# Later loads, split stores and readings, and a later meeting of q and k in a two-layer decoder kernel

## The chip, the cores and the metric

The kernel runs on one core of one Trainium2 chip. Its time is the device time of one execution in microseconds, the median of the runs shown. A core has a matrix engine (PE, with its weight loads listed apart as PEld), a vector engine (DVE), a scalar engine (ACT), a general one (POOL) and an engine that here only issues transfers (SP). Each of them executes its own instructions in the order in which the program emits them; semaphores tie them together.

## The reference

Two decoder layers over 256 positions of width 2048, in float32, with a final RMSNorm. Each layer norms its input, multiplies it by one wide input matrix, mixes the heads, gates the result and multiplies it by an output matrix:

```python
def layer_even(x, norm_g, w_in, w_out):        # layer 0
    h = rmsnorm(x, norm_g)
    qa, ka, va, iq, ik, iw, qb, kb, vb, gate = split_cols(h @ w_in, SPLIT0)
    ...                                        # rotary embedding of q and k
    o_a = dsa_attention(qa, ka, va, iq, ik, iw)    # 10 heads, 64 keys chosen by an indexer
    o_b = dilated_attention(qb, kb, vb)            # 6 heads, three dilated windows merged
    y = concatenate([o_a, o_b])
    return x + (y * silu(gate)) @ w_out

def layer_odd(x, norm_g, w_in, b_f, w_out):    # layer 1
    h = rmsnorm(x, norm_g)
    qc, kc, vc, qd, kd, vd, fl, gate = split_cols(h @ w_in, SPLIT1)
    o_c = stick_breaking_attention(qc, kc, vc)     # 8 heads
    o_d = forgetting_attention(qd, kd, vd, log_f)  # 8 heads, softmax with forget bias
    y = concatenate([o_c, o_d])
    return x + (y * silu(gate)) @ w_out
```

All heads are 128 wide. The weights are about 160 MB of float32 and are read once.

## The kernel before

**Projections.** The work is a list of 39 jobs (lines 228 to 231): 14 of layer 0 (B0, K, I0, I1, B1 and so on; a B job is one head's q, k, v and gate, 512 columns; an A job is the q and gates of two heads; K holds the shared key and value, I0 and I1 the indexer's queries), four output jobs P0 to P3, 17 of layer 1 (C and D heads, with C1 cut in F1 and G1 of about half width), and Q0 to Q3. `project` runs a job over 16 blocks of the contraction (kt) for both halves of the positions (th). Precision comes from splitting every operand in a high and a low part, so each block takes six matmuls: lines 316, 317 and 319, twice. The weights arrive in pieces of four blocks (1 MB at full width) in three buffers with the tag "raw" (line 252). `split` cuts half a piece at a time: ACT writes the high part `whi` (line 280), DVE the low part `wlo` (line 281), each in four buffers. The splits run three halves ahead of the matmuls (`AHEAD`, line 310). When the second half of a piece has been put in line, `split` calls `load` for a further piece (line 284).

**Ticks.** Everything else is woven into the projections by hand. A piece of side work is a generator that yields the number of ticks it wants to wait; a tick is one block of a job at full width, six matmuls (lines 304 to 308 and 336). `advance` resumes the generators that are due, oldest first. So a tick sets only the place of an instruction in its engine's queue; when it executes is up to the queue and the semaphores. In these pages, tick 0 of a head is the end of its projection, and tick 16 is the end of the next one of full width.

**A head.** At tick 0 the head's opening work takes q, k, v and the gate out of PSUM (`scaled_qk`, `vg1` in layer 1; `rotate` in layer 0). q and k have to be turned (transposed) for their product, and so has the gate u. That goes through DRAM, by `far` (line 400): DVE transposes blocks of 32 by 32 (line 410), a store writes them out (line 411), a reading brings them back in the wanted order (line 413). `qk_turned` then cuts q and k in parts (`qk_parts`, ACT lines 388 and 389, DVE line 390), which is called "parts" below; A heads do the same in lines 709 to 711. One or two ticks later q meets k in a matmul (line 486 for A, B and D, line 853 for C). What follows in a softmax head is the row minimum and exponential (`soft`, lines 492 and 494), `share`, the turning of the weights on PE (`turn`, line 380), the cut into ph and pl, and `weigh_out`, which multiplies with v and with the turned gate and writes the head's columns of y. A C head (`stick_head`) has a logarithm and a running sum by matmul (lines 865 to 868) in the place of the softmax.

In ticks of a D head, before the change: qk transposed and stored at 2, u at 5, qk read back at 5, u at 9, parts at 9, meeting at 10, weigh_out at 17. Heads A and B meet at 11. The last heads before an output job, B5 and D7 (`last`), turn q and k on PE instead, and their gate through DRAM with shorter waits.

**Transfers.** Nearly all of them are issued by SP, in order: loads of weights, stores and readings of turned blocks, the residual x (lines 259 and 260). An instruction at the head of SP's queue that waits holds those behind it. Several tiles share a tag with few buffers: "qk" has two (q and k of a head, the indexer's `iqr`, the key `kr`, the turned residual `xf`).

**feed1** (line 761) turns the residual after each P job the same way, as input of layer 1, and **keys_a** (line 601) the shared key of the A heads.

Of the kernel before, what the change touches and what calls it, by code (L numbers as in the profile page):

```python
# [14 lines left out]
P = 128  # L15
# [31 lines left out]
def _run_of(base, h):  # L47
    return np.arange(base + h * HD, base + (h + 1) * HD)
# [11 lines left out]
def _cols0(n):  # L60
    qa, ka, va, iq, ik, iw, qb, kb, vb, g = O0
    h = int(n[1:] or 0)
    if n == "K":
        p = [_inter(ka, HD), _run_of(va, 0), _inter(ik, DI), np.arange(iw, iw + NI)]
    elif n[0] == "I":
        p = [_inter(iq + (8 * h + i) * DI, DI) for i in range(8)]
    elif n[0] == "B":
        p = [_inter(qb + h * HD, HD), _inter(kb + h * HD, HD), _run_of(vb, h), _gate_of(g, HA + h)]
    else:
        p = [_inter(qa + h * HD, HD), _inter(qa + (h + 1) * HD, HD), _gate_of(g, h), _gate_of(g, h + 1)]  # L70
    return np.concatenate(p)


def _cols1(n):
    qc, kc, vc, qd, kd, vd, fl, g = O1
    h = int(n[1:])
    if n[0] == "F":
        p = [_run_of(qc, h), _run_of(kc, h), np.arange(fl, fl + HDD)]
    elif n[0] == "G":
        p = [_run_of(vc, h), _gate_of(g, h)]  # L80
    elif n[0] == "C":
        p = [_run_of(qc, h), _run_of(kc, h), _run_of(vc, h), _gate_of(g, h)]
    else:
        p = [_run_of(qd, h), _run_of(kd, h), _run_of(vd, h), _gate_of(g, HC + h)]
    return np.concatenate(p)


# [84 lines left out]
def trunk(ctx, tc, x, xT, g1, w0, wo0, w1, wo1, bf, gf, consts, rope, out):  # L172
# [68 lines left out]
    def load():  # L241
        i = st["load"]
        if i == len(pieces):
            return
        st["load"] += 1
        wd, off, n, w = pieces[i]
        if i < len(FIRST):

            kt = sum(FIRST[:i])
            raws[i] = home[kt // 8][:, (kt % 8) * w:(kt % 8 + n) * w]  # L250
        else:
            raws[i] = wp.tile([P, n * w], F32, name="raw", tag="raw")
        if i == 1 or 3 < i < len(FIRST):
            load_xT(kt)
        nc.sync.dma_start(raws[i], wd[off:off + P * n * w].rearrange("(p f) -> p f", p=P))
        if i in (0, 2):
            load_xT(i)
        if i == len(FIRST) + 1:
            for th in range(NT):
                nc.sync.dma_start(xs[:, th, :], x[th * P:(th + 1) * P, :])  # L260
            nc.sync.dma_start(rt.rearrange("p a b -> p (a b)"), rope)
        if i == len(FIRST) + 2:
            nc.sync.dma_start(cons, consts)

    def split(upto):
        while st["split"] < min(upto, len(halves)):
            i = st["split"]
            st["split"] += 1
            ji, pi, kt, j0, m = halves[i]
            w = pieces[pi][3]  # L270
            if jobs[ji][2] == "Q3" and kt < 8:
                hi = xh.rearrange("p a b -> p (a b)")[:, kt * w:(kt + m) * w]
                lo = xl.rearrange("p a b -> p (a b)")[:, kt * w:(kt + m) * w]
            else:
                hi = wp.tile([P, m * w], F32R, name="whi", tag="whi", bufs=4)
                lo = wp.tile([P, m * w], F32R, name="wlo", tag="wlo", bufs=4)
            if ji == 0:
                feed0(kt, m)
            rw = raws[pi][:, j0 * w:(j0 + m) * w]
            nc.scalar.activation(hi, rw, AF.Copy)  # L280
            nc.vector.tensor_tensor(lo, rw, hi.bitcast(F32), op=OP.subtract)  # L281
            parts[i] = (hi, lo)
            if (i + 1 == len(halves) or halves[i + 1][1] != pi) and (pi >= len(FIRST) - 1 or kt + m == 10):
                load()


    side = []
# [16 lines left out]
    def tick(w):  # L304
        clock["t"] += w / 512
        if clock["t"] >= 0.99:
            clock["t"] -= 1.0
            advance(1)

    AHEAD = 3  # L310
    hidx = [0]
# [85 lines left out]

        return t.rearrange("p (i b c) -> p b i c", i=4, b=n)

    def far(srcs, dst, first, between):  # L400

        yield first
        t = hp.tile([P, 512], F32, name="far", tag="rt2")
        ns = [x.shape[1] // P for x in srcs]
        n = sum(ns)
        d = dr.tile([P, P * n], F32, name="fard", tag=f"fard{n}", bufs=4)
        o = t[:, 0:P * n].rearrange("p (j b c) -> p b j c", j=4, b=n)
        for i, x in enumerate(srcs):
            b = sum(ns[:i])
            nc.vector.transpose(o[:, b:b + ns[i]], x.rearrange("p (b j l) -> p b j l", j=4, l=32))  # L410
        nc.sync.dma_start(d, t[:, 0:P * n])
        yield between
        nc.sync.dma_start(dst.rearrange("p (i f) -> p i f", i=4),
                          d.rearrange("r (j f) -> (r j) f", j=4).rearrange("(i q) f -> q i f", i=4))

    def qk_turned(qk, first, last):

        if last:
            yield first + 1
            r = qk_parts(quarters(turn([qk[:, i * P:(i + 1) * P] for i in range(4)])))  # L420
            yield 1
        else:
            yield from far([qk], qk, first, 3)
            yield 4
            r = qk_parts(arrived(qk, 4))
        yield 1
        return qk_of(r)

# [31 lines left out]
            upper(th)  # L460
        return (vh, vl, v1), upper, lower

    def gate_turned(u, last=False, n=NT):
        uT = hp.tile([P, P * n], F32, name="uT", tag="uT" if n == NT else "rl")
        start(far([u], uT, 1 if last else 5, 3 if last else 4))
        return arrived(uT, n)

    def weigh_out(ph, pl, p1, v, uT, kt, swap):

# [37 lines left out]
        for th, s in BLK:  # L507
            nc.vector.tensor_scalar(pr[:, s], pr[:, s], sc[:, th:th + 1], None, op0=OP.mult)

    def softmax_head(qk, nb, v, uT, rs, kt, last):  # L510
        pr, l = soft(qk, nb)
        yield 2
        share(pr, factor(l, rs))
        yield 2 if last else 3
        pt = turn([pr[:, 0:P], pr[:, P:SEQ], pr[:, SEQ:384]])
        ph = hp.tile([P, SEQ], F32R, name="ph", tag="ph", bufs=1)
        pl = hp.tile([P, SEQ], F32R, name="pl", tag="pl", bufs=1)
        p1 = hp.tile([P, P], F32, name="p1", tag="p1", bufs=1)
        cut((ph, pl), pt[:, 0:SEQ])
        nc.scalar.activation(p1, pt[:, SEQ:384], AF.Copy)  # L520
        yield 2
        weigh_out(ph, pl, p1, v, uT, kt, False)

# [56 lines left out]
    def head_b(ps, h):  # L580
        qk = hp.tile([P, 512], F32, name="qk", tag="qk")
        v, upper, lower = values(ps, 256, r0, ())
        u = hp.tile([P, SEQ], F32, name="u", tag="u")
        tg = hp.tile([P, SEQ], F32, name="tg", tag="tg")
        for th in range(NT):

            rotate(qk[:, th * 256:(th + 1) * 256], ps[th][:, 0:256], rt[:, th, 0:256], rt[:, th, 256:512], 1, 256,
                   swap=th == 1)
            o = 1 - th
            nc.scalar.activation(tg[:, o * P:(o + 1) * P], ps[o][:, 384:512], AF.Tanh, scale=hr0[:, o:o + 1])  # L590
            upper(o)
        for th in (1, 0):
            t = slice(th * P, (th + 1) * P)
            nc.vector.scalar_tensor_tensor(u[:, t], tg[:, t], 1.0, ps[th][:, 384:512], op0=OP.add, op1=OP.mult)
        lower()
        last = h == HB - 1
        uT = gate_turned(u, last)
        t = yield from qk_turned(qk, 3, last)
        yield from softmax_head(t, bmask, v, uT, hr0, YPOS[f"B{h}"], last)

    def keys_a(ps):
        kr = hp.tile([P, 512], F32, name="kr", tag="qk")
# [11 lines left out]
        for j in range(2):  # L614
            d = slice(j * DI, (j + 1) * DI)
            c = slice(SEQ + j * P, SEQ + (j + 1) * P)
            for t in (ikh, ikl):
                nc.gpsimd.tensor_copy(t[d, c], t[d, 0:P].bitcast(F32))
        yield from far([kr[:, 0:256]], kr[:, 0:256], 1, 3)
        yield 4  # L620
        k = arrived(kr[:, 0:256], 2)
        nc.scalar.activation(quarters(kA), k[:, 0:1], AF.Copy)
        nc.scalar.activation(quarters(kAh), k, AF.Copy)
# [66 lines left out]
    def heads_a(ps, h):  # L690
# [7 lines left out]
        for th in (1, 0):  # L698
            nc.vector.scalar_tensor_tensor(u[:, :, th, :], tgs[th].rearrange("p (a b) -> p a b", a=2), 1.0,
                                           ps[th][:, 256:512].rearrange("p (a b) -> p a b", a=2),  # L700
                                           op0=OP.add, op1=OP.mult)
        uT = gate_turned(u.rearrange("p a b c -> p (a b c)"), n=4)
        yield from far([qk], qk, 3, 3)
        yield 4
        q = arrived(qk, 4)
        f = hp.tile([P, 256], F32, name="qqf", tag="qkf", bufs=1)
        hi = hp.tile([P, 256], F32R, name="qqh", tag="qkh", bufs=1)
# [1 line left out]
        nc.scalar.activation(quarters(hi), q[:, 2:4], AF.Copy)  # L709
        nc.scalar.activation(quarters(f), q[:, 0:2], AF.Copy)  # L710
        nc.vector.tensor_tensor(quarters(lo), q[:, 2:4], quarters(hi).bitcast(F32), op=OP.subtract)
        yield 1
        js = [slice(j * P, (j + 1) * P) for j in range(2)]

        ph, pl = (hp.tile([P, 2, SEQ], F32R, name="pA" + n, tag="i" + n, bufs=1) for n in "hl")
# [45 lines left out]
    def feed1(ps, c):  # L761
        residual(ps, 1, c)
        us = [hp.tile([P, 512], F32, name="xf", tag="qk") for _ in range(2)]
        for i, t in enumerate(us):
            k = (c * 4 + 2 * i) * P
            start(far([xs[:, th, k:k + 2 * P] for th in range(NT)], t, 1 + i, 3))
        yield 4
        if c == 3:
            norm(1)
# [108 lines left out]

    def stick(qk, v, u, kt):
        uT = gate_turned(u)  # L880
        t = yield from qk_turned(qk, 2, False)
        yield from stick_head(t, v, uT, kt)

    def head_c(ps, h):
# [8 lines left out]
    def head_d(ps, h):  # L893
        qk = scaled_qk(ps, 1, (0, 3), (1, 2))
        v, u = vg1(ps, 256)
        last = h == HDD - 1
        uT = gate_turned(u, last)
        t = yield from qk_turned(qk, 2, last)
        yield from softmax_head(t, biases[h], v, uT, None, HC + h, last)


    def tail(ps, c2):
# [131 lines left out]
```

## Time and profile before

| what | value |
|---|---|
| median of the runs shown | 1050.57 us (1042.25 to 1053.46) |
| the profiled execution, its own time | 1054.77 us |
| its span, first to last instruction | 1053.0 us |
| mean granted clock of PE in it | 0.942 |
| DMA moved | 194.72 MB, mean 185 GB/s |
| instructions | 11945 |

The profile belongs to one execution. Its views list, for each engine, the busy time (a busy PE is not a PE at full speed, since it also counts matmuls at a lower clock), groups of instructions by source line with count, total and mean duration, who waited for whom, and the instructions in order of time. A row of the timeline reads: start, duration, engine, line, operation, output and input tile, shapes, count, and in square brackets how long the engine had been idle and what released it. A row of the table of stretches reads: from and to, length, busy time with the number of instructions for PE, PEld, DVE, ACT and POOL, then PE's granted clock, the busy share of the DMA engines, and GB/s. In the list of waits a row reads: engine, waiting tile and line, what it waited for, total us, times, longest.

### The profile page before, as it was taken

Reading aid. Unit: us, or ns where it says so; the run is one execution under the profiler, and the core shown is the slowest. Engines: PE = TensorE matmul, PEld = TensorE weight load, DVE = VectorE, ACT = ScalarE, POOL = GpSimd, SP = SyncE. Lnnn points to the kernel's source line nnn. Section 1 sums busy time; section 2 is a strip of 40 time slices with the busy share of each in tenths; the row PEclk is TensorE's granted clock in tenths of the full one; section 3 lists DMA queues with packets and bytes.
Section 4 is the critical chain, followed back from the end, with each engine's and each line's share of the span. In section 5 each row is a group of like instructions: output and inputs, shape, how many; then the busy total and the mean of one; then the engine's idle time right before and its main releaser. Section 6 shows DMA issues by size and latency. Waiting matters only on the chain.

```text
span 1053.0 us, 11945 instructions
## 1 busy us (share of the span) xinstructions
PE 941.6 (89%) x4291; PEld 778.1 (74%) x4291; DVE 651.9 (62%) x1138; ACT 481.6 (46%) x832; POOL 50.2 (5%) x71
## 2 busy tenths in 40 slices
PE   9999998998988899999978889887878977879997
PEld 6878877776767688878866667776666766767886
DVE  6678877566666666667645566564556644657554
ACT  6645544444444455454544444444333433445441
POOL 0131000000000000000000000000000000000010
PEclk9999999999999999999988899898889888989999
DMA  9944455556555546665655553445655346454452
GB/s 368 342 161 158 156 203 174 179 195 200 200 166 194 190 156 206 210 239 170 233 190 156 184 190 127 150 150 195 197 185 166 125 140 191 158 185 166 171 193 80
DMA packets 68123, 194.72 MB, mean 185 GB/s; under 512 B 16976, under 2 KB 39904, under 8 KB 49888
## 3 DMA queue, kind: packets, MB, share of 16 engines
q1 hardware_dynamic: 66624, 190.66, 53.4%
q0 software_dynamic: 864, 2.12, 1.2%
q10 hardware_dynamic: 576, 1.19, 0.3%
q8 instruction: 33, 0.54, 0.2%
q14 instruction: 26, 0.21, 0.1%
HBM read 178.87 MB, written 15.08 MB: 184 GB/s over the span
## 4 chain that ended last, share of the span: by engine, by line
PE 43%; DMA 29%; DVE 14%; ACT 9%; issue 5%; SPq 0%; POOL 0%; DVEq 0%; POOLq 0%; ACTq 0%
DMA qk<-fard 14%; PE pj L316 13%; PE pj L317 12%; PE pj L319 12%; DMA fard<-far 10%; DVE wlo L281 5%; ACT whi L280 3%; DVE e L805 3%; DVE far L410 2%; DMA xf<-fard 2%; PE s L486 1%; DMA xs<-in_x_dram 1%; DMA raw<-in_w_in_dram 1%; ACT e L802 1%; ACT qkh L388 1%
## 5 line engine op out<-in xcount | busy, mean ns | idle before, releaser
L281 DVE TENSOR_TENSOR wlo<-raw,whi 128x1024 fp32r<-128x1024 f32 (+3 forms) x300 | 355.2, 1198 | 141.6 <-ACT whi L280 139.0
L316 PE MATMUL pj<-whi,xh 128*128 128x512 f32 (+3 forms) x992 | 396.8, 401 | 0.2
L317 PE MATMUL pj<-whi,xl 128*128 128x512 f32 (+3 forms) x992 | 391.9, 396 | 0.0
L280 ACT ACTIVATE whi<-raw 128x1024 fp32r<-128x1024 f32 (+3 forms) x300 | 300.0, 1023 | 108.6 <-PE pj L317 89.5
L319 PE MATMUL pj<-wlo,xh 128*128 128x512 f32 (+3 forms) x992 | 307.0, 392 | 0.5 <-DVE wlo L281 0.4
L316 PEld LDWEIGHTS pj<-whi,xh 128*128 128x128 f32 x992 | 196.4, 198 | 37.2 <-ACT whi L280 2.2
L319 PEld LDWEIGHTS pj<-wlo,xh 128*128 128x128 f32 x992 | 192.2, 197 | 41.2 <-DVE wlo L281 1.6
L317 PEld LDWEIGHTS pj<-whi,xl 128*128 128x128 f32 x992 | 196.1, 198 | 34.8 <-DVE xl L564 0.2
L316 PE MATMUL pj<-whi,yh 128*128 128x512 f32 (+1 forms) x248 | 95.9, 387 | 0.0
L317 PE MATMUL pj<-whi,yl 128*128 128x512 f32 (+1 forms) x248 | 95.0, 383 | 0.0
L319 PE MATMUL pj<-wlo,yh 128*128 128x512 f32 (+1 forms) x248 | 76.9, 383 | 0.1
L390 DVE TENSOR_TENSOR qkl<-qk,qkh 128x384 fp32r<-128x384 f32 x20 | 11.2, 558 | 89.2 <-ACT qkh L388 89.2
L388 ACT ACTIVATE qkh<-qk 128x384 fp32r<-128x384 f32 x20 | 10.4, 522 | 107.9 <-DMA qk<-fard 107.9
L486 PE MATMUL s<-qkf 128*128 128x128 f32 x28 | 8.9, 412 | 52.8 <-ACT qkf L389 52.7
L319 PEld LDWEIGHTS pj<-wlo,yh 128*128 128x128 f32 x248 | 46.5, 188 | 9.8 <-DVE wlo L281 0.7
L316 PEld LDWEIGHTS pj<-whi,yh 128*128 128x128 f32 x248 | 46.6, 188 | 9.0 <-ACT whi L280 0.3
L317 PEld LDWEIGHTS pj<-whi,yl 128*128 128x128 f32 x248 | 46.7, 188 | 8.7
L443 ACT ACTIVATE yh<-uT 128x256 fp32r<-128x256 f32 (+1 forms) x27 | 12.4, 457 | 82.6 <-DVE uT L479 36.0
L486 PEld LDWEIGHTS s<-qkf 128*128 128x128 f32 x28 | 5.6, 248 | 58.4 <-ACT qkf L389 58.3
L494 ACT ACTIVATE sn<-sn,nm 128x128 f32<-128x128 f32 (+1 forms) x48 | 21.5, 448 | 44.1 <-DVE nm L492 44.1
L853 PE MATMUL s<-qkf 128*128 128x128 f32 x16 | 6.1, 480 | 34.8 <-ACT qkf L389 34.8
L853 PEld LDWEIGHTS s<-qkf 128*128 128x128 f32 x16 | 3.8, 296 | 38.0 <-ACT qkf L389 38.0
(226 smaller groups left out, 791.2 us busy)
## 6 DMA issues: line engine op xcount, KB each, us to landing
raw<-in_w_in_dram SPq DMA_DIRECT2D x108, 1024.0 KB, 5.2
raw<-in_w_out_dram SPq DMA_DIRECT2D x32, 1024.0 KB, 5.0
fard<-far SPq DMA_DIRECT2D x38, 256.0 KB, 5.2
qk<-fard SPq DMA_DIRECT2D x25, 256.0 KB, 6.4
fard<-far SPq DMA_DIRECT2D x23, 128.0 KB, 5.7
uT<-fard SPq DMA_DIRECT2D x22, 128.0 KB, 3.7
raw<-in_w_in_dram SPq DMA_DIRECT2D x4, 672.0 KB, 9.6
raw<-in_w_in_dram SPq DMA_DIRECT2D x4, 528.0 KB, 3.7
```

The source lines that it names most:

```text
L280: nc.scalar.activation(hi, rw, AF.Copy)
L281: nc.vector.tensor_tensor(lo, rw, hi.bitcast(F32), op=OP.subtract)
L316: nc.tensor.matmul(o, a, wh, start=(kt == 0), stop=False)
L317: nc.tensor.matmul(o, b, wh, start=False, stop=False)
L319: nc.tensor.matmul(o, a, wl, start=False, stop=(kt == KT - 1))
L388: nc.scalar.activation(quarters(hi), blocks[:, 1:4], AF.Copy)
L390: nc.vector.tensor_tensor(quarters(lo), blocks[:, 1:4], quarters(hi).bitcast(F32), op=OP.subtract)
L410: nc.vector.transpose(o[:, b:b + ns[i]], x.rearrange("p (b j l) -> p b j l", j=4, l=32))
L443: nc.scalar.activation(dst[0], src, AF.Copy)
L486: nc.tensor.matmul(pS[:, 0:P], q0, k0, start=True, stop=True)
L494: nc.scalar.activation(sn[:, s], sn[:, s], AF.Exp, scale=-1.0, bias=nm[:, th:th + 1], accum_out=l[:, th:th + 1])
L805: nc.vector.reciprocal(e, e)
```

## The change

- `split` puts the load of the next piece of weights in line four ticks later, except during the first job.
- `far` takes three numbers: the ticks before DVE's transposition, from there to the store, and from the store to the reading. Before, the store stood right behind the transposition.
- In heads B, C and D qk is transposed at tick 2, stored at 4 and read at 8; parts are at 15 and the meeting at 18. A heads have the same. u is transposed at 4, stored at 6, read at 10. `keys_a` and `feed1` use the three numbers too; from the start of its turning, the key is ready for use after 12 ticks instead of 8.
- The gates of B5 and D7 are no longer stored and read: PE turns them, with two transposes and an ACT copy each, beside the turning of the softmax weights. Their columns of the weights are left in plain order for it. The meeting of D7 comes one tick later (6).
- x is loaded in six transfers instead of two.

```diff
@@ load
             for th in range(NT):
-                nc.sync.dma_start(xs[:, th, :], x[th * P:(th + 1) * P, :])
+                for c0, c1 in ((0, 768), (768, 1536), (1536, D)):
+                    nc.sync.dma_start(xs[:, th, c0:c1], x[th * P:(th + 1) * P, c0:c1])
@@ split
-                load()
+                load() if ji == 0 else start(later(load, 4))
+    def later(f, n):
+        yield n
+        f()
@@ far
-    def far(srcs, dst, first, between):
+    def far(srcs, dst, first, done, stored):
...
+        yield done
         nc.sync.dma_start(d, t[:, 0:P * n])
-        yield between
+        yield stored
         nc.sync.dma_start(dst.rearrange("p (i f) -> p i f", i=4),
...
@@ qk_turned
-    def qk_turned(qk, first, last):
+    def qk_turned(qk, last):
         if last:
-            yield first + 1
+            yield 4
             r = qk_parts(quarters(turn([qk[:, i * P:(i + 1) * P] for i in range(4)])))
             yield 1
         else:
-            yield from far([qk], qk, first, 3)
-            yield 4
+            yield from far([qk], qk, 2, 2, 4)
+            yield 7
             r = qk_parts(arrived(qk, 4))
+            yield 2
         yield 1
@@ gate_turned
-        start(far([u], uT, 1 if last else 5, 3 if last else 4))
+        start(far([u], uT, 4, 2, 4))
+    def gate_turned_here(u):
+        pt = turn([u[:, 0:P], u[:, P:SEQ]])
+        uT = hp.tile([P, SEQ], F32, name="uT", tag="uT")
+        nc.scalar.activation(uT, pt[:, 0:SEQ], AF.Copy)
+        return quarters(uT)
@@ softmax_head
-    def softmax_head(qk, nb, v, uT, rs, kt, last):
-        pr, l = soft(qk, nb)
+    def softmax_head(qk, nb, v, u, rs, kt, last):
+        uT = None if last else gate_turned(u)
+        qk = yield from qk_turned(qk, last)
+        pr, l = soft(qk, nb() if callable(nb) else nb)
...
+        if last:
+            uT = gate_turned_here(u)
         yield 2
         weigh_out(ph, pl, p1, v, uT, kt, False)
@@ keys_a
-        yield from far([kr[:, 0:256]], kr[:, 0:256], 1, 3)
-        yield 4
+        yield from far([kr[:, 0:256]], kr[:, 0:256], 1, 2, 4)
+        yield 5
@@ heads_a
-        yield from far([qk], qk, 3, 3)
-        yield 4
+        yield from far([qk], qk, 2, 2, 4)
+        yield 7
...
-        yield 1
+        yield 3
@@ feed1
-            start(far([xs[:, th, k:k + 2 * P] for th in range(NT)], t, 1 + i, 3))
+            start(far([xs[:, th, k:k + 2 * P] for th in range(NT)], t, 1 + i, 1, 3))
```

More of the change, by code (lines that the diff above doesn't have):

```diff
@@ L67, in _cols0 @@
     elif n[0] == "B":
-        p = [_inter(qb + h * HD, HD), _inter(kb + h * HD, HD), _run_of(vb, h), _gate_of(g, HA + h)]
+        p = [_inter(qb + h * HD, HD), _inter(kb + h * HD, HD), _run_of(vb, h),
+             (_run_of if h == HB - 1 else _gate_of)(g, HA + h)]
     else:
@@ L83, in _cols1 @@
     else:
-        p = [_run_of(qd, h), _run_of(kd, h), _run_of(vd, h), _gate_of(g, HC + h)]
+        p = [_run_of(qd, h), _run_of(kd, h), _run_of(vd, h),
+             (_run_of if h == HDD - 1 else _gate_of)(g, HC + h)]
     return np.concatenate(p)
@@ L461, in values, with gate_turned @@
         return (vh, vl, v1), upper, lower
-    def gate_turned(u, last=False, n=NT):
+    def gate_turned(u, n=NT):
         uT = hp.tile([P, P * n], F32, name="uT", tag="uT" if n == NT else "rl")
-        start(far([u], uT, 1 if last else 5, 3 if last else 4))
+        start(far([u], uT, 4, 2, 4))
         return arrived(uT, n)
+    def gate_turned_here(u):
[3 more added lines that the diff above has]
+        return quarters(uT)
     def weigh_out(ph, pl, p1, v, uT, kt, swap):
@@ L596, in head_b @@
         last = h == HB - 1
-        uT = gate_turned(u, last)
-        t = yield from qk_turned(qk, 3, last)
-        yield from softmax_head(t, bmask, v, uT, hr0, YPOS[f"B{h}"], last)
+        yield from softmax_head(qk, bmask, v, u, hr0, YPOS[f"B{h}"], last)
     def keys_a(ps):
@@ L701, in heads_a @@
                                            op0=OP.add, op1=OP.mult)
-        uT = gate_turned(u.rearrange("p a b c -> p (a b c)"), n=4)
-        yield from far([qk], qk, 3, 3)
-        yield 4
+        uT = gate_turned(u.rearrange("p a b c -> p (a b c)"), 4)
+        yield from far([qk], qk, 2, 2, 4)
+        yield 7
         q = arrived(qk, 4)
@@ L880, in stick @@
         uT = gate_turned(u)
-        t = yield from qk_turned(qk, 2, False)
+        t = yield from qk_turned(qk, False)
         yield from stick_head(t, v, uT, kt)
@@ L896, in head_d @@
         last = h == HDD - 1
-        uT = gate_turned(u, last)
-        t = yield from qk_turned(qk, 2, last)
-        yield from softmax_head(t, biases[h], v, uT, None, HC + h, last)
+        yield from softmax_head(qk, lambda: biases[h], v, u, None, HC + h, last)
     def tail(ps, c2):
```

## The prediction

> **What bounds the kernel now.** I read the head of the page first, then the list of who waited for whom, then the timeline around one head, then a table of stretches with their clock.
>
> ```profile
> PE 941.6 (89%) x4291; PEld 778.1 (74%) x4291; DVE 651.9 (62%) x1138; ACT 481.6 (46%) x832; POOL 50.2 (5%) x71
> core 0: 1053.0 us, clock 0.942
> ...
> 425.00:450.00 25.00, 24.93 (x110) 20.11 (x109) 14.23 (x22) 11.71 (x19) 0.00 (x0) 1.00 0.67 221
> 584.00:615.00 31.00, 26.59 (x112) 21.79 (x111) 17.96 (x27) 13.89 (x24) 0.00 (x0) 0.89 0.47 161
> ```
>
> PE is the busiest engine, yet it idles 1053.0 - 941.6 = 111.4 us, and its mean clock of 0.942 is another loss. The stretch 425:450 shows it unhindered: 110 matmuls in 25 us at full clock, so a tick of six costs 25 / 110 x 6 = 1.36 us. DMA moves 221 GB/s there, above any head of layer 1, and PE does not notice. The 31 us of head C (584:615) held nearly the same count at a clock of 0.89.
>
> ```profile
> ACT qkh L388 <- DMA qk<-fard: 107.9, 19, 8.0
> PE s L486 <- ACT qkf L389: 52.7, 12, 6.9
> PE s L853 <- ACT qkf L389: 34.8, 8, 6.4
> PE s L486 <- ACT qqf L710: 14.2, 5, 4.2
> ...
> 804.99 0.33 SPq L411 DMA_DIRECT2D fard<-far  x1
> 807.25 0.33 SPq L255 DMA_DIRECT2D raw<-in_w_in_dram  x1
> 808.95 0.38 SPq L413 DMA_DIRECT2D qk<-fard  x1
> ...
> 818.09 0.80 PE L486 MATMUL s<-qkf 128*128 128x128 f32 x2 [6.39 <-ACT qkf L389]
> ```
>
> Nearly all of PE's idle time stands in front of one kind of matmul, the meeting of q and k: 52.7 + 34.8 + 14.2 = 101.7 us in 25 places. The cause is the block turned through DRAM: in this D head the store goes out at 804.99, the reading may only start when it has landed (808.95), and PE goes on at 818.09. PE executes in order, so everything behind this matmul stands too.
>
> ```profile
> 54.70:62.70 8.00, 8.00 (x32) 6.48 (x33) 4.50 (x13) 3.50 (x8) 1.94 (x4) 0.79 0.31 123
> 140.90:148.90 8.00, 7.97 (x38) 6.32 (x39) 5.50 (x18) 3.66 (x7) 0.00 (x0) 1.00 0.33 96
> 818.20:826.20 8.00, 8.00 (x26) 6.55 (x27) 3.83 (x10) 2.99 (x6) 0.00 (x0) 0.64 0.05 17
> 943.50:951.50 8.00, 8.00 (x31) 6.69 (x32) 3.82 (x10) 3.53 (x7) 0.00 (x0) 0.79 0.04 11
> ```
>
> The stall has an echo. These are the 8 us after four of the 25 meetings (first, second, one D head, last): PE is busy throughout, but at 0.79 or 0.64 it issues 26 to 32 matmuls instead of 38. Over all 25 such rows the missing clock is 5.63, which times 8 us is 45.0 us.
>
> **The change, part by part.**
>
> *q and k meet at tick 18* (before: 10 in heads C and D, 11 in A and B). That is 7 or 8 ticks, 9.5 to 10.9 us, more than the longest wait shown (6.9 us). In the D head above, store to meeting took 13.1 us; now 14 ticks, 19 us, lie between the store's place (4) and the meeting (18). Gain: up to 101.7 us of idle time and 45.0 us of clock. 1053.0 - 101.7 - 45.0 = 906.3 us.
>
> *What is late next.* A head's meeting (tick 18) now falls on tick 2 of the following head, right behind that head's opening work on DVE. A meeting at full clock, the opening of an A head, and a C head:
>
> ```profile
> 140.78 0.49 PE L486 MATMUL s<-qkf 128*128 128x128 f32 x2 [1.31 <-ACT qkf L389]
> 141.46 0.40 PE L316 MATMUL pj<-whi,xh 128*128 128x512 f32 x1
> ...
> 319.84 0.41 DVE L369 TENSOR_TENSOR rot<-pj,rt 128x256 f32<-128x256 f32 x1
> 322.08 2.39 DVE L281 TENSOR_TENSOR wlo<-raw,whi 128x1024 fp32r<-128x1024 f32 x2 [0.17 <-ACT whi L280]
> ...
> 632.13 0.56 DVE L856 TENSOR_TENSOR z<-s,cons 128x384 f32<-128x384 f32 x1 [1.24 <-PE s L432]
> 635.53 0.56 DVE L444 TENSOR_TENSOR spl<-sp,sph 128x384 fp32r<-128x384 f32 x1 [0.59 <-ACT sph L443]
> 640.81 0.34 PE L865 MATMUL s<-sph,tris 128*128 128x384 f32 x1
> 643.07 0.61 ACT L791 ACTIVATE qk<-pj,rr 128x128 f32<-128x128 f32 x2
> 645.16 1.75 DVE L805 RECIPROCAL e<-e 128x256 f32<-128x256 f32 x1
> 647.73 1.22 DVE L281 TENSOR_TENSOR wlo<-raw,whi 128x1024 fp32r<-128x1024 f32 x1
> 648.87 0.70 DVE L410 STREAM_TRANSPOSE far<-qk 128x512 f32<-128x512 f32 x1
> ```
>
> Count from 643.07, the first reading of a finished projection. DVE is through the opening and one split at 648.95, 5.9 us. From z to the end of spl takes 3.96 us, so spl is ready at 9.8. PE reaches the matmul that needs it (line 865) at tick 7: 7 x 1.36 + 0.68 for the meeting (140.78 to 141.46) = 10.2. It fits with 0.4 us to spare. Behind it DVE has the turning of qk (0.70), splits B, C and D (1.22 each) and the turning of u (0.44), to 15.1, then z and pl with ACT's two steps between, about 2.0, so 17.1. weigh_out needs pl at tick 11: 10.2 + 0.6 + 4 x 1.36 = 16.2. PE waits 0.9 us. A D head does the same sum without the chain of ACT (share ready at 10.3 against 10.2, pl 0.4 late). I take 0.7 us for each of the 15 heads of layer 1: 10.5 us; ends are 0 and one more split with its ACT step ahead of z, 2.3 us each, 34 us. A and B open with 2.2 us of DVE (319.84 to 322.08) instead of 4.7, so they have room: 0.3 each, 3 us, ends 0 and 10.
>
> *The weights' loads four ticks later in line.*
>
> ```profile
> SPq L255 <- DVE wlo L281: 442.5, 88, 11.0
> SPq L413 <- DMA fard<-far: 111.1, 50, 5.0
> ACT whi L280 <- DMA raw<-in_w_in_dram: 8.7, 6, 2.4
> ...
> raw<-in_w_in_dram SPq DMA_DIRECT2D x108, 1024.0 KB, 5.2
> raw<-in_w_in_dram SPq DMA_DIRECT2D x4, 672.0 KB, 9.6
> fard<-far SPq DMA_DIRECT2D x38, 256.0 KB, 5.2
> qk<-fard SPq DMA_DIRECT2D x25, 256.0 KB, 6.4
> ```
>
> SP is ahead: it spends 442.5 us standing at a load until DVE frees the buffer. A place further back only means that stores and readings put in those ticks go first. Behind the load nothing urgent waits; in front of it now stand a store (its transposition was put two ticks before, so no wait) or a reading, which waits for its store, 111.1 / 50 = 2.2 us each. From the split that frees a buffer to the split that needs the new piece are ten ticks, 13.6 us. If the load really went 4 ticks later, 8.2 us remained: enough for 5.2, 1.4 short for the worst row, 9.6. So 0 for full-width pieces. F1 and G1 are half as wide, ten ticks are five there, and C0's readings fall on them: 3 us, between 0 and the 8.7 us that ACT waits for weights in the whole run now.
>
> *Stores and readings apart.* The same DMAs in the same number; the store no longer holds SP while DVE transposes. The readings are put at tick 8 (qk) and 10 (u), and in practice go when the store has landed. By the C row, turning now ends near 10.6; plus 5.2 and 6.4 is 22.2, and parts are put at tick 15, near 22. ACT may stand a microsecond or two there; the meeting is three ticks (4.1 us) further. Zero, as long as that cover holds; without it, each microsecond counts 25 times.
>
> *keys_a* reads kr at tick 30 of the count in which index already takes kr's slot at 26 (two "qk" slots, the other is free). POOL's second sum, row below, starts only after that reading, and PE wants it at 31: about 1.2 + 1.77 - 1.36 = 1.6 us, once; ends 0 and 3.
>
> ```profile
> L375 POOL TENSOR_TENSOR iqr<-rot,rot 128x512 f32<-128x512 f32 x4 | 7.0, 1766 | 30.7 <-DVE rot L370 20.3 <-issue 10.4
> L410 DVE STREAM_TRANSPOSE far<-u 128x256 f32<-128x256 f32 (+1 forms) x27 | 13.1, 487 | 0.0
> L380 PE MATMUL tp<-cons,sn 128*128 128x128 f32 x72 | 11.9, 273 | 0.0
> L443 ACT ACTIVATE ph<-tp 128x256 fp32r<-128x256 f32 x14 | 5.4, 386 | 21.1 <-PE tp L380 21.1
> ```
>
> *Gates of B5 and D7 turned on PE.* Away: two stores, two readings, two transpositions of DVE (0.49). New: four PE transposes (at most 0.27 each, 1.1 us in all) and two ACT copies (0.39). The result is wanted at kt 15 of the next projection and is put at tick 12, so three ticks hide it. PE's 1.1 us are counted: 1. D7's meeting is one tick later, under the same cover. *feed1* puts its reading a tick later, consumption stays at tick 8: 0, P shows no stall to lengthen. *x in six pieces*: four more issues of 0.33 us on SP early on, hidden by pieces already loaded: 0, between -3 and 1.3. The column order of two gates costs nothing.
>
> Sum: 906.3 + 10.5 + 3 + 3 + 1.6 + 1 = 925.4 us span. The profiled run took 1054.77 us, 1.8 over its span, and stands 0.4% above the median of 1050.57; so (925.4 + 1.8) x 1050.57 / 1054.77 = 923 us.
>
> **Two rules against the rows.** The gap of 1.31 us at the second meeting was followed by full clock (140.90 above). This one of 1.89 us was not:
>
> ```profile
> 194.75 0.49 PE L486 MATMUL s<-qkf 128*128 128x128 f32 x2 [1.89 <-ACT qkf L389]
> ...
> 194.90:202.90 8.00, 8.00 (x31) 6.53 (x32) 4.73 (x12) 3.74 (x7) 0.00 (x0) 0.79 0.31 88
> ```
>
> It cost 0.21 x 8 = 1.7 us more. So leftover gaps of about 2 us are priced with an echo, and those under 1 us without. The Trainium skill, TensorE: Matmul & The Clock Gate, section "Why this matters for your kernels", puts the limit at idle gaps over some 3 us; by it leftovers of 2 us would cost their own length alone, and rival 1 below would come out 13 us lower. The rows decide here.
>
> PE busy, 941.6 us, looks like a floor; in that reading the gain ends at 111.4 us. The four stretches contradict it, being fully busy at 26 to 38 matmuls. The Trainium skill, Trainium Kernel Development and Optimization, section "Performance Expectations", calls matmul busy time a bad metric and weight loading the better one; by the 778.1 us of PEld the room would be 275 us. The rows agree with it as far as that time below 941.6 can be reached.
>
> **The rivals.**
>
> 1. *DVE becomes the bound in layer 1.* A C head used 17.96 us of DVE in 31, plus its waits for ACT and PE (1.24 and 0.59 above are two of them); the new head has 16 x 1.36 + about 2 = 24 us. If z waits one more split, each of 15 heads keeps a gap of 2.3 us, half of them with the echo: 15 x (2.3 + 0.85) = 47, and 10 in layer 0: 906.3 + 57 + 5.6 + 1.8 = 971, as median 967. For: my margin is 0.4 us. Against: DVE's splits run three halves ahead.
> 2. *The clock does not come back* though the gaps shrink: 1053.0 - 101.7 + 19.1 = 970 span, 968 us. Against: 425:450.
> 3. *Weights arrive late: slower.* If SP really issues four ticks late, a buffer's turn is 5.4 us + landing + two pieces' use and split. Three buffers then feed a piece every (5.4 + L + 5.4) / 3 us. There are 152 such pieces (38 projections by four), now one per 6.9 us, so it decides from L = 10 us on; at 11 us, 7.3 x 152 = 1105 us. For: the 9.6 row. Against: 5.2 us in 108 loads.
> 4. *The wait only moves along*: the turned block lands as much later as the meeting does, since store and reading have moved too. Then 1050 us. Against: the landing of the store, not the place, let the reading go at 808.95.
>
> **How the numbers follow.** As forecast 0.69 (its own range 903 to 945); first rival 0.19; second 0.05; third 0.04; fourth 0.03. A measurement here tells about 1% from no change. Faster by over 1%: 0.93, the first three together; within: 0.03; slower: 0.04. The range goes from 900, a little under the 904 that all extra costs at zero would give ((906.3 + 1.8) x 0.996), to 966, just short of rival 1's full price; it leaves out half of rivals 1 and 2, and 3 and 4 whole.
>
> **What would show it.** The three rows "PE s" fall from 101.7 to under 15 us; the clock rises to 0.98 or more; 31 us per layer-1 head become about 25; the idle time of qkh shrinks but need not vanish. PE waiting for pl or sph in front of lines 865 or 430 speaks for rival 1; ACT waiting for raw for over 30 us for rival 3. The forecast is wrong if a wait behind the opening work of the next head is over 2 us.

## The result, and the profile after

The changed kernel takes 911.64 us (median of 4 runs, 911.52 to 915.88), the kernel before 1052.01 us beside it. The ratio is 0.869, with a 95% interval of 0.863 to 0.875. The forecast was 923 us with a range of 900 to 966. The profiled execution took 911.52 us, its span is 909.7 us.

The head of the page, the core's line, and from the table of stretches one projection of the C heads (546 to 570 us); columns as before: length, busy time of PE, PEld, DVE, ACT and POOL, clock, DMA share, GB/s.

```profile
PE 893.6 (98%) x4295; PEld 748.1 (82%) x4295; DVE 647.1 (71%) x1136; ACT 479.8 (53%) x834; POOL 49.3 (5%) x71
core 0: 909.7 us, clock 0.997
...
546.00:570.00 24.00, 24.00 (x113) 20.12 (x112) 17.79 (x27) 13.66 (x23) 0.00 (x0) 1.00 0.60 210
```

PE's idle time fell from 111.4 us to 909.7 - 893.6 = 16.1, of which 8.3 us lie at the two ends of the run. The clock rose from 0.942 to 0.997. PE's busy time itself is 48 us shorter although the program has four matmuls more: before, many of them ran at half clock. A C head, 31 us before, now fits in 24 us in which PE never pauses. DVE does about the same work in it, 17.8 us (17.96 before).

From the list of who waited for whom, all rows in which PE's matmuls wait for 0.6 us or more, and the landing times of the DMA list:

```profile
PE tp L388 <- DVE sn L524: 1.8, 1, 1.8
PE s L502 <- ACT qkf L397: 1.5, 1, 1.5
PE s L959 <- DVE mhalf L955: 1.2, 1, 1.2
PE s L441 <- DVE qkl L398: 1.1, 2, 0.7
PE s L883 <- ACT sph L453: 0.8, 1, 0.8
PE tp L388 <- POOL kr L625: 0.7, 1, 0.7
PE o L441 <- DVE pl L454: 0.6, 1, 0.6
...
raw<-in_w_in_dram SPq DMA_DIRECT2D x108, 1024.0 KB, 5.4
fard<-far SPq DMA_DIRECT2D x38, 256.0 KB, 2.2
qk<-fard SPq DMA_DIRECT2D x25, 256.0 KB, 3.4
```

The meeting of q and k (line 502, before 486) held PE for 101.7 us in 25 places and now for 1.5 us in one, with 1.1 us more in two places at the low part of the product (line 441). ACT's wait for the turned block, 107.9 us before, has left the list. Two things are new. The stores land in 2.2 us instead of 5.2 and the readings in 3.4 instead of 6.4, which the forecast had not expected. And SP now waits elsewhere:

```profile
SPq L420 <- DVE far L418: 328.8, 58, 13.0
SPq L257 <- DVE wlo L284: 221.8, 65, 8.1
SPq L422 <- DMA fard<-far: 52.1, 38, 5.7
```

Before, SP stood 442.5 us at loads until a split was done (line 255) and 46.4 us at stores. Now it stands 328.8 us at stores (line 420), with loads behind it, and 221.8 us at loads until a split is done.

The hand schedule of a C head, against its rows after (chosen rows of DVE, ACT and PE in order of time; 546.42 is ACT's first reading of the finished projection):

```profile
551.03 1.22 DVE L284 TENSOR_TENSOR wlo<-raw,whi 128x1024 fp32r<-128x1024 f32 x1
552.16 0.55 DVE L874 TENSOR_TENSOR z<-s,cons 128x384 f32<-128x384 f32 x1
555.01 0.53 ACT L453 ACTIVATE sph<-sp 128x384 fp32r<-128x384 f32 x1 [0.63 <-DVE sp L879]
555.57 0.56 DVE L454 TENSOR_TENSOR spl<-sp,sph 128x384 fp32r<-128x384 f32 x1 [0.59 <-ACT sph L453]
556.56 0.34 PE L883 MATMUL s<-sph,tris 128*128 128x384 f32 x1
556.56 0.19 PEld L884 LDWEIGHTS s<-spl,tris 128*128 128x128 f32 x1
558.13 2.32 DVE L284 TENSOR_TENSOR wlo<-raw,whi 128x1024 fp32r<-128x1024 f32 x2
561.96 0.42 DVE L893 TENSOR_TENSOR pl<-z,ph 128x256 fp32r<-128x256 f32 x1 [1.04 <-ACT ph L891]
562.63 0.28 PE L440 MATMUL o<-ph,v 128*128 128x256 f32 x1
```

The opening work and one split end at 552.25, 5.8 us in (forecast 5.9); spl is ready at 556.13, 9.7 us in (9.8); PE gets to line 883 at 10.1 us (10.2). Line 883 itself reads sph, which is ready at 555.54, 1.0 us ahead of it; spl is read by line 884, whose weight load starts together with line 883. So the chain fits, with 0.4 us to spare for spl, as worked out, and 1.0 for sph. pl is ready at 562.38, 16.0 us in, where the forecast had 17.1, and PE reaches weigh_out at 16.2.

### The profile page after: what moved, and what is told of

The parts are those of the page before. It is cut to its first block, busy times and chain, and to the rows that moved or that the text cites. A ratio compares the mean times of both kernels' runs of the same rounds, so it can differ in the third digit from the quotient of the medians.

```text
span 909.7 us, 11956 instructions
## 1 busy us (share of the span) xinstructions
PE 893.6 (98%) x4295; PEld 748.1 (82%) x4295; DVE 647.1 (71%) x1136; ACT 479.8 (53%) x834; POOL 49.3 (5%) x71
## 4 chain that ended last, share of the span: by engine, by line
PE 82%; DMA 7%; DVE 5%; ACT 2%; issue 2%; POOL 1%; SPq 0%; POOLq 0%; DVEq 0%; ACTq 0%
PE pj L324 25%; PE pj L325 25%; PE pj L327 25%; DMA raw<-in_w_in_dram 6%; DVE wlo L284 2%; PE tp L388 1%; ACT whi L283 1%; DMA xst<-in_xT_dram 1%; DVE e L823 1%; PE s L502 1%; PE o L441 1%; PE s L441 1%; PE o L489 1%; DMA w0yh<-in_w_in_dram 0%; PE s L442 0%
## 5 line engine op out<-in xcount | busy, mean ns | idle before, releaser
L324 PE MATMUL pj<-whi,xh 128*128 128x512 f32 (+3 forms) x992 | 381.3, 386 | 0.6 <-ACT whi L283 0.5
L325 PE MATMUL pj<-whi,xl 128*128 128x512 f32 (+3 forms) x992 | 376.8, 381 | 0.0
L327 PE MATMUL pj<-wlo,xh 128*128 128x512 f32 (+3 forms) x992 | 297.1, 381 | 0.4 <-DVE wlo L284 0.4
L324 PEld LDWEIGHTS pj<-whi,xh 128*128 128x128 f32 x992 | 186.8, 188 | 33.6 <-ACT whi L283 1.7
L325 PEld LDWEIGHTS pj<-whi,xl 128*128 128x128 f32 x992 | 186.9, 188 | 32.1
L546 ACT ACTIVATE sq<-xs 128x512 f32<-128x512 f32 x23 | 14.3, 624 | 28.9 <-DVE xs L769 26.8
L823 DVE RECIPROCAL e<-e 128x256 f32<-128x256 f32 x16 | 28.1, 1754 | 0.5
L383 POOL TENSOR_TENSOR qk<-rot,rot 128x256 f32<-128x256 f32 x16 | 11.6, 739 | 228.9 <-DVE rot L378 182.3
L454 DVE TENSOR_TENSOR yl<-uT,yh 128x256 fp32r<-128x256 f32 (+1 forms) x27 | 12.8, 475 | 14.3 <-ACT yh L453 14.3
L809 ACT ACTIVATE qk<-pj,rr 128x128 f32<-128x128 f32 x32 | 10.0, 362 | 16.0 <-PE pj L327 16.0
```

Of the source, the lines that this page charges most:

```text
L324: nc.tensor.matmul(o, a, wh, start=(kt == 0), stop=False)
L325: nc.tensor.matmul(o, b, wh, start=False, stop=False)
L327: nc.tensor.matmul(o, a, wl, start=False, stop=(kt == KT - 1))
L383: nc.gpsimd.tensor_tensor(dst, t1[:, 0:n], t2[:, 0:n], op=OP.add)
L454: nc.vector.tensor_tensor(dst[1], src, dst[0].bitcast(F32), op=OP.subtract)
L546: nc.scalar.activation(j, xs[:, th, c * 512:(c + 1) * 512], AF.Square, accum_out=ss[:, i, th, c:c + 1])
```

## The experiments

Times are medians; ratios are to the kernel before, run beside each. The changed kernel is called "the change".

**The meeting alone.** The kernel before with only the ticks of parts and meeting moved:

```diff
             yield from far([qk], qk, first, 3)
-            yield 4
+            yield 12 - first
             r = qk_parts(arrived(qk, 4))
+            yield 2
...
         yield from far([qk], qk, 3, 3)
-        yield 4
+        yield 9
         q = arrived(qk, 4)
...
-        yield 1
+        yield 3
         js = [slice(j * P, (j + 1) * P) for j in range(2)]
```

> The kernel before, with the meeting of q and k alone moved to tick 18 (parts at 15) in all heads but B5 and D7; loads, stores and readings stand in line as before. Theory M (the place of the meeting is what gains: 7 or 8 ticks of cover): 910 to 930 us, the three rows of PE waiting at the meeting fall from 101.7 to under 15 us, clock 0.98 or more, while the store still lands in about 5 us and the reading in about 6. Theory O (the order of SP's queue gains, because turned blocks no longer go behind a 1 MB load): the round trip stays long and the wait moves along, 980 us or more.

Measured: 908.43 us (907.89 to 908.96), ratio 0.864 [0.861, 0.867]. The rows of PE waiting for turned q and k are down to 1.0 us, and store and reading land in 4.6 and 5.4 us, a little sooner than before (5.2 and 6.4). So the place of the meeting is worth the whole gain without any reordering of SP's queue.

**The loads alone.** The kernel before with the loads of weights four ticks later in line:

```diff
-                load()
+                load() if ji == 0 else start(later(load, 4))
```

> The kernel before, with the loads of weights alone put in line four ticks later; the meeting stays at 10 or 11, the store right behind the transposition. Theory M: within 3% of before (1020 to 1060 us), since the meeting has no more ticks of cover. Theory O: store and reading land in about 2.2 and 3.4 us as in the changed kernel, the waits at the meeting fall by more than half, 980 us or less.

Measured: 955.9 us, ratio 0.909 [0.906, 0.912]. Theory M fell here: this alone takes 95 us off. The lists of waits and of DMAs of this kernel, and two rows of SP's timeline in a D head:

```profile
PE s L490 <- ACT qkf L393: 18.5, 12, 4.5
PE s L857 <- ACT qkf L393: 17.6, 8, 4.2
PE s L490 <- ACT qqf L714: 6.0, 5, 1.4
...
fard<-far SPq DMA_DIRECT2D x38, 256.0 KB, 2.1
qk<-fard SPq DMA_DIRECT2D x25, 256.0 KB, 3.8
...
715.13 0.33 SPq L415 DMA_DIRECT2D fard<-far  x1
715.55 0.38 SPq L255 DMA_DIRECT2D raw<-in_w_in_dram  x1
```

The store now goes out before the 1 MB load, not behind it, and lands in 2.1 us instead of 5.2. Before, a load of weights was in flight when the store went in 60 of 61 places; here it is in 25 of 61. At the readings of qk one is in flight in all 25 places in both kernels, but it was issued longer ago (2.6 us in the median instead of 1.7). The round trip of the turned block shrinks from 5.2 + 6.4 = 11.6 us to 5.9, and PE's wait at the meetings from 101.7 to 42.1 us. The meeting alone and the loads alone are thus two remedies for the same wait: one gives the block more time, the other makes it faster.

**The change without its later loads.**

```diff
-                load() if ji == 0 else start(later(load, 4))
+                load()
```

> The changed kernel with the loads of weights put in line at once, as before the change. Theory M: within 1% of 912 us; landing of store and reading goes back to about 5 and 6 us, and the four ticks between parts and meeting hide it. Theory O: over 935 us, with PE waiting at the meeting again.

Measured: 907.82 us (907.24 to 908.67), ratio 0.863 [0.860, 0.866]. Store and reading land in 4.8 and 5.4 us again, and the ticks up to 18 hide it. It is the same as the meeting alone and 3.8 us under the change; no run of the two overlaps. Once the meeting stands at 18, the later loads cost a little.

**The change with the store right behind its transposition.**

```diff
-        yield done
         nc.sync.dma_start(d, t[:, 0:P * n])
-        yield stored
+        yield done + stored
```

> The changed kernel with each store put in line right behind its transposition, the reading at the same tick as in the change. Theory M: within 0.5% of 912 us, SP waits for DVE at the store as it does anyway (328.8 us in the changed kernel). Theory O: SP stands at the store with loads behind it, over 920 us.

Measured: 917.53 us (916.6 to 921.57), ratio 0.873 [0.870, 0.876], so 6 us over the change (the lowest run here is 916.6, the highest of the change 915.88): between the two theories' numbers, and more than M allowed. SP waits at the stores about as long as in the change (333.9 us, 328.8), so the longer standing at the store that theory O expected is not in the rows. What differs in the rows is the order behind the stores: the last load goes 0.5 us ahead of qk's reading (median) instead of 3.3, the readings land in 5.5 us instead of 3.4, the 1 MB loads in 6.0 instead of 5.4, and ACT's wait for weights grew from 23.0 us to 36.2. That this order makes the 6 us is not shown by a run of its own. In the profiled executions a gap of 1.8 us that PE has in both kernels is followed by half clock here (at 683.04, a clock of 0.79 over 8 us, so 1.7 us) and not in the change, which makes a part of them.

**Stores apart alone.** The kernel before with the store two ticks behind its transposition and the reading one tick later:

```diff
+        yield 2
         nc.sync.dma_start(d, t[:, 0:P * n])
-        yield between
+        yield between - 1
...
-            yield 4
+            yield 3
             r = qk_parts(arrived(qk, 4))
```

> The kernel before, with the stores alone put two ticks behind their transposition and the readings one tick later than before; meeting and loads as before. Theory S (what counts is whether a load stands in front of the store or behind it): loads still stand in front, store and reading land in about 5 and 6 us, 1035 to 1075 us. If it is the wait of SP at the store for DVE that held the kernel: 1000 us or less.

Measured: 1059.23 us, ratio 1.0073 [1.0044, 1.0102]. By itself this part makes the kernel slightly slower. The store still follows a load (landing 5.9 us), and PE waits 54.8 + 32.1 + 17.9 = 104.8 us at the meetings.

**The meeting back at 10, the rest of the change kept.**

```diff
             yield from far([qk], qk, 2, 2, 4)
-            yield 7
+            yield 1
             r = qk_parts(arrived(qk, 4))
-            yield 2
         yield 1
```

The A heads have the same: 1 tick to the parts and 1 to the meeting.

> The changed kernel with the meeting back at tick 10 (parts at 9) in all heads; loads later, stores and readings apart stay. So far the place of the meeting alone gave 908 us and the later loads alone 956 us. Theory S (two remedies for one wait, each nearly enough by itself): 940 to 985 us, like the later loads alone, with gaps of 1 to 3 us at each meeting, since the reading now stands only two ticks before the meeting. Theory T (the change needs all its parts together): above 1000 us.

Measured: 936.6 us (934.27 to 941.78), ratio 0.893 [0.889, 0.898], a little under the band. PE waits 27.1 us at meetings (15.9 in B and D, 11.2 in C). With the faster round trip even tick 10 keeps most of the gain. It is also 19 us less than with the loads alone; which of the other parts brings that was not taken apart.

**The meeting at 14**, with one tick between parts and meeting (two in A):

```diff
             yield from far([qk], qk, 2, 2, 4)
-            yield 7
+            yield 4
             r = qk_parts(arrived(qk, 4))
-            yield 2
+            yield 1
```

> The changed kernel with the meeting at tick 14 (parts at 12, reading at 8 as in the change). The reading lands in about 3.4 us, 2.5 ticks, so parts can start near tick 11 to 12. Theory S: 908 to 920 us, no gap over 1 us at most meetings. If the turned block needs all the ticks up to 18: 925 us or more.

Measured: 940.14 us, ratio 0.896 [0.892, 0.900]. The expectation of 908 to 920 fell, and more ticks than at 10 did not help. PE does not wait at any meeting; it waits later in the head. The list of waits, and one C and one D head in the timeline:

```profile
PE o L441 <- DVE pl L454: 13.9, 9, 2.1
PE o L440 <- ACT ph L891: 11.2, 8, 1.9
...
571.40 0.38 PE L440 MATMUL o<-ph,v 128*128 128x256 f32 x1 [1.32 <-ACT ph L891]
...
721.82 0.39 PE L441 MATMUL o<-pl,v 128*128 128x256 f32 x1 [1.66 <-DVE pl L454]
```

With the meeting at 14, weigh_out stands at tick 5 (D) or 7 (C) of the following head, and what it needs, ph and pl, is behind that head's opening work on ACT and DVE.

**The meeting at 14, weigh_out where the change has it:** four ticks more before it, in all heads but the last ones.

```diff
-        yield 2
+        yield 2 if last else 6
         weigh_out(ph, pl, p1, v, uT, kt, False)
```

C and A heads have 7 for 3 at the same place.

> The changed kernel with the meeting at tick 14 as in the run at 940 us, but weigh_out put four ticks later, at the tick that it has in the change (25 in B and D, 27 in C, 29 in A). In the run at 940 us PE waited in front of weigh_out for ph and pl, whose work on ACT and DVE falls on the opening work of the next head. Theory W (tick 14 is enough for the turned block; what cost there is where the later steps of the head fall): 907 to 918 us, PE's waits at weigh_out gone. Rival (tick 14 itself is too early): 930 us or more.

Measured: 907.78 us (907.66 to 909.28), ratio 0.865 [0.862, 0.867]. The waits at weigh_out are gone and the 32 us with them. One C head waits at its meeting, 1.9 us. So with loads behind the stores the turned block needs hardly more than tick 14. What the rest of the delay to 18 buys is that the steps behind the meeting fall beside the opening work, not under it.

**PE kept busy in the gap.** The kernel before with matmuls that serve nothing in front of each meeting (8 in A and B, 20 in C, 30 in D), overwritten by the meeting:

```diff
+        for _ in range(pad):
+            nc.tensor.matmul(pS, xh[:, 0, 0:P], xh.rearrange("p a b -> p (a b)")[:, 0:384], start=True, stop=True)
         nc.tensor.matmul(pS[:, 0:P], q0, k0, start=True, stop=True)
```

> The kernel before, with useless matmuls of 384 columns in front of each meeting (8 in heads A and B, 20 in C, 30 in D; 0.18 us each at full clock) that fill the gap in which PE waits for the turned q and k; nothing else is moved, and their result is overwritten. Theory E (the half clock after a gap is caused by PE's idleness and costs real time): the idle time turns into busy time, the clock goes to 0.97 or more, and the time falls by 25 to 45 us, to 1005 to 1030, although PE has more to do. Rival (the clock column costs nothing, the gap is all): 1045 to 1065 us.

Measured: 1020.98 us, ratio 0.973 [0.967, 0.978]. The same q and k come as late as before (ACT waits 107.7 us for them), PE has 450 matmuls more to do, and the kernel is 29 us faster. PE still waits 9.8 + 9.5 + 7.0 = 26.3 us at the meetings, where the added matmuls do not fill the gap. From the page, the core's line, and the timeline at one D head:

```profile
PE 984.7 (96%) x4741; PEld 832.1 (81%) x4741; DVE 649.3 (64%) x1138; ACT 480.7 (47%) x832; POOL 50.2 (5%) x71
core 0: 1021.2 us, clock 0.987
...
821.96 5.39 PE L487 MATMUL s<-xh 128*128 128x384 f32 x30
827.18 0.38 PE L488 MATMUL s<-qkf 128*128 128x128 f32 x2
...
827.76 0.40 PE L316 MATMUL pj<-whi,xh 128*128 128x512 f32 x1
...
829.15 0.39 PE L316 MATMUL pj<-whi,xh 128*128 128x512 f32 x1
```

After the meeting a tick takes 829.15 - 827.76 = 1.39 us at once. So the echo is a cost of PE's idleness, not of the data.

**More work on DVE.** The change with the gate's reciprocal done three times in each head of layer 1, the value unchanged up to rounding:

```diff
-        nc.vector.reciprocal(e, e)
+        for _ in range(3):
+            nc.vector.reciprocal(e, e)
```

> The changed kernel with the reciprocal of the gate (1.75 us of DVE) done three times in each of the 16 heads of layer 1, 3.5 us more of DVE in the opening work. Theory D (in layer 1 the chain behind the opening work has about 0.4 us to spare at line 883 of the changed kernel): PE waits some 3 us there in C heads and at the turning in D heads, 15 x 3 = 45 us and echoes, 950 to 985 us. Rival (the splits run three halves ahead and absorb it): under 925 us.

Measured: 983.74 us, ratio 0.937 [0.932, 0.942]. 16 x 3.5 = 56 us of DVE cost 72 us. The list of waits and the timeline of a C head:

```profile
PE s L884 <- ACT sph L453: 19.7, 8, 2.5
PE tp L388 <- DVE sn L524: 18.0, 6, 3.1
...
549.03 0.69 PE L884 MATMUL s<-sph,tris 128*128 128x384 f32 x1 [2.44 <-ACT sph L453]
...
550.53 0.63 PE L324 MATMUL pj<-whi,xh 128*128 128x512 f32 x1
550.96 0.63 PE L325 MATMUL pj<-whi,xl 128*128 128x512 f32 x1
```

PE waits where the theory had put it, 2.4 us in C and up to 3.1 us in D. In a C head that is the 3.5 us more, less the 1.0 us that sph had to spare. Most gaps bring their echo: the last two rows start 0.43 us apart, the same two lines of the projection 0.24 in the change (557.14 and 557.38), and the clock of the whole run is 0.967. DVE as a whole is busy 72%; still what goes beyond the margin at this place comes out as a wait of PE, with the echo on top.

**The collision.** The change with the 1 MB of the last norm's gains loaded after D3 instead of D1:

```diff
-        if name == "D1":
+        if name == "D3":
             for c in range(2):
                 gb.append(hp.tile([P, 1024], F32, name="gb", tag=("ih", "il")[c], bufs=1))
```

> The changed kernel with the 1 MB load of the last norm's gains, which POOL issues after D1 is projected, issued after D3 instead. In the changed kernel this load is in flight while the store of D0's gate is; SP stands at that gate's reading until 661.24, the next load of weights goes only then, ACT waits 5.3 us for it and PE has two gaps of 1.7 and 2.0 us. If the collision is the cause: 907 to 910 us, or the two gaps reappear two heads later and the time is the same. If the loads' later place costs by itself everywhere: 911 to 912 us with other gaps in their place.

Measured: 908.03 us (906.01 to 908.09), ratio 0.864 [0.861, 0.866]. This is what it mends, in the timeline of the change:

```profile
652.70 1.10 POOL L990 DMA_DIRECT2D gb<-in_norm_f_dram  x2 [168.19 <-PE s L886]
...
653.61 0.33 SPq L420 DMA_DIRECT2D fard<-far  x1
...
661.24 0.37 SPq L422 DMA_DIRECT2D uT<-fard  x1
661.71 2.35 SPq L257 DMA_DIRECT2D raw<-in_w_in_dram  x2
...
667.78 1.06 ACT L283 ACTIVATE whi<-raw 128x1024 fp32r<-128x1024 f32 x1 [5.34 <-DMA raw<-in_w_in_dram]
```

POOL issues the gains at 652.70, and they take 7.3 us to land (median of the two), so the gate's store of 653.61 is in flight with them. Its reading, and the load of weights behind that, go only at 661. ACT waits 5.34 us for the weights, and PE has gaps of 1.5 and 1.8 us (the first two rows of the list of waits after the change). With the gains later these gaps are gone, and the kernel is 3.6 us faster, the same as the one with its loads at once. That one has the collision too: there the same gate's store goes at 654.89 and its reading only at 665.08, but the next load stands ahead of the reading (659.33), and PE has no such gap. So it takes both, the gains beside the store and a load held behind the reading. The later loads cost here and nowhere else that shows.

**The two last gates and x.** The change with the gates of B5 and D7 through DRAM again, and x in two pieces:

```diff
-        uT = None if last else gate_turned(u)
+        uT = gate_turned(u, NT, last)
...
-                for c0, c1 in ((0, 768), (768, 1536), (1536, D)):
+                for c0, c1 in ((0, D),):
```

> The changed kernel with the gates of B5 and D7 turned through DRAM again (their columns permuted again) and x loaded in two pieces. The forecast charged PE 1.1 us for the turning and nothing for the rest: 909 to 913 us, no difference over 0.3%. Rival (the removed transfers freed something on the path): 914 us or more.

Measured: 911.54 us (910.11 to 912.06), ratio 0.867 [0.865, 0.869]: the same as the change.

## Why the prediction was right

The forecast was 923 us in 900 to 966; 911.6 was measured. Its sum was built in the right order, and its largest terms held.

1. *What bounded the kernel.* The wait of PE at the meetings (101.7 us) and its echo (45.0 us) were read from the profile before, and taking them off gave a span of 906.3 us. The span after is 909.7. PE's busy time fell by 48.0 us, close to the price of the echo. The run with busy gaps shows that the echo is real, the run with the meeting alone that the wait goes where the forecast said.
2. *What is late next.* The schedule of a C head met line 883 within 0.1 us. One reading in it was wrong: line 865 (883 after) needs sph, and the line behind it spl. The 0.4 us hold all the same, for the weight load of spl; sph has 1.0, and the run with 3.5 us more of DVE work, where PE waits 2.4 us for sph, agrees. The wait of 0.9 us at weigh_out was wrong. It took 15.1 us for the end of split D, and even its own addends (9.8 + 0.70 + 3 x 1.22 + 0.44) give 14.6. Back to back, the splits start 1.1 us apart, since two take 2.32 us together, so z could start at 14.0, and did (560.37, 13.95 us in). The 10.5 us charged to layer 1, and the 3 us for heads A and B, did not come; outside the collision PE's rows after have 0.8 us at sph and 0.6 us at pl in all.
3. *The key and the indexer*, charged 1.6 us: PE waited 0.7 us for kr and not for iqr. *F1 and G1*, charged 3 us: the row at sph, 0.8 us, is all that stands out near them. ACT waits 9.9 us for weights there, between 459 and 475 us (4.5 us before, at 498 to 501), and PE goes on.
4. *The mis-sized step* is thus the sum of leftovers, 19.1 us forecast; 909.7 - 906.3 = 3.4 us were measured, of which the collision makes about as much.
5. *The later loads were priced at 0, and that was wrong in its reason.* I wrote "Behind the load nothing urgent waits". The store and the reading of the turned block wait there: with the stores in front of a 1 MB load, store and reading land in 2.1 and 3.8 us, with the stores behind it in 5.2 and 6.4. Alone the step is worth 95 us. In the change it adds nothing to the moved meeting, so the forecast's total did not suffer, which was luck, and in one place it costs 3.6 us. That place is the third rival's mechanism in small: SP held at a reading, the weights behind it late.
6. *The rivals.* DVE as the bound did not come; with 3.5 us more of DVE work in each head of layer 1 it did, with gaps of 2.4 to 3.1 us and 983.7 us in all (the rival's price was 967 for gaps of 2.3). The clock came back. The fourth rival named the right weakness, that more ticks help only if the block arrives no later; with loads in front it arrived as before, which was enough.
7. *The reason for tick 18.* I took all 7 or 8 ticks as cover for the turned block. The two runs at 14 show that with the loads behind the stores four ticks do for the block, but for one wait of 1.9 us, and that the place of weigh_out decides the rest.

The time went below PE's old busy time of 941.6 us, which thus was no floor. The Trainium skill, Trainium Kernel Development and Optimization, section "Performance Expectations", calls matmul busy time a bad metric. The trace agrees: PE is busy 893.6 us now, for four matmuls more, and what shortened it here is the clock.

The best versions run here are four that do not differ: the kernel before with the meeting alone (908.4 us), the change with its loads at once (907.8), the change with the gains loaded later (908.0), and the meeting at 14 with weigh_out late (907.8).

## What to carry to other kernels

Where an in-order matrix engine stands in front of one kind of matmul, move that matmul later in the program until its input is surely there, and count the gap twice: once as idle time, once for the matmuls at half clock behind it. Then place the steps behind it against what the vector engine has in line at that time, step by step with durations from the trace; an engine that is busy 71% of the run can have 0.4 us to spare at the place that counts. A small urgent transfer belongs in front of a large one in its issuing queue, and a change made of several parts should be run part by part, since two of them may cure the same wait.

## What the runs showed of the hardware

In these runs the landing of a store depended on what was issued just before it on the same queue. A store of 256 KB took 5.2 us behind a load of 1 MB and 2.1 us in front of it, in the same kernel but for the order. What another queue has in flight counts too: beside POOL's 1 MB of gains SP's store of 653.61 let its reading go only after 7.6 us. The Trainium skill, DMA: Bandwidth & Descriptors, section "Queues, rings and completion order", says that each DMA engine consumes the descriptors of one issuing queue in ring order. The rows of SP's stores and loads agree with it.

Half clock after a gap is not a matter of its length alone. In the kernel with the loads alone, PE waited 2.32 us at a meeting and went on at full clock for the 10 us behind it (timeline of a late head, and two rows of the table of stretches, clock third from the end):

```profile
847.09 0.49 PE L490 MATMUL s<-qkf 128*128 128x128 f32 x2 [2.32 <-ACT qkf L393]
```

```profile
846.00:850.00 4.00, 2.91 (x15) 2.54 (x16) 1.20 (x5) 2.52 (x7) 0.00 (x0) 1.00 0.89 309
850.00:858.00 8.00, 8.00 (x40) 6.63 (x39) 5.25 (x10) 4.57 (x11) 0.00 (x0) 1.00 0.44 157
```

In the kernel before, 1.89 us at 194.75 cost an echo. With tripled reciprocals two C heads have the same gap of 2.44 us, ending at 549.03 and at 576.96; the first has an echo and the second has none:

```profile
549.00:557.00 8.00, 7.97 (x30) 6.45 (x31) 6.42 (x9) 5.39 (x7) 0.00 (x0) 0.80 0.77 257
577.00:585.00 8.00, 7.83 (x36) 6.27 (x37) 6.43 (x9) 5.39 (x7) 0.00 (x0) 1.00 0.77 253
```

Over the traces of all the runs, PE's gaps of 1.8 to 2.6 us were followed by a lower clock in 13 of 29 places. So the forecast's price for leftover gaps of about 2 us, one echo in two, was about right on the whole; the runs do not settle what decides in a single place, nor from which length on an echo is sure.
